# A decoder block on one core: the token norm applied by the transposes, and the first convolution chunk computed in turns over four banks

## The chip, the cores and the metric

The kernel runs on one core of a Trainium2 chip. The metric is the device time of one execution in microseconds (us); the smaller the better. The engines of the core work side by side, each through its own row of instructions in order: TensorE (PE) multiplies, VectorE (DVE), ScalarE (ACT) and GpSimd (POOL) do the elementwise work, SyncE (SP) issues the transfers from memory.

## The reference

The kernel computes one decoder block for 256 tokens of width 1024, in float32. The parts that the change touches stand first.

```python
h = rmsnorm(x, norm_mix_g)
proj = h @ w_in                       # q, k, v, forget gate, conv value a, conv gate
a, gate = split(proj[..., OFF_C:] + b_glu)
z = a * sigmoid(gate)                 # 512 channels
z = depthwise_causal_conv(z, w_dw) + b_dw        # width 31
conv = silu(layernorm(z, ln_g, ln_b))
attn = rmsnorm(forgetting_attention(q, k, v, log_sigmoid(f)))
x = x + concat([attn, conv]) @ w_out
x = x + memory_cross_attention(rmsnorm(x), rmsnorm(mem), w_mq, w_mkv, w_mo)
x = x + hierarchical_moe(rmsnorm(x), ...)        # 4 groups of 8 experts, top 2
out = rmsnorm(x)
```

## The kernel before

**Weights and the ring.** Weights pass through a ring of 15 slots in the on-chip memory. SP issues their loads in the order of `ring.queue`; `ring.pump` issues as many as slots are free, and a slot comes free when PE has used its content. The first conv weights, `("ca", 0)` (value) and `("cg", 0)` (gate), `("ca", 1)` and `("cg", 1)`, are queued first. The normed tokens `xn` hold one slot-sized place until they are transposed.

**Products in three parts.** A float32 product is made of three single-pass ones (`mm3`, L415 to L417): both factors are split into a high and a low part, and high x high, high x low and low x high are added up in a PSUM bank. The weight's split is made by `split` in pieces of 128x512: ACT casts the high part `WH` (L409), and GpSimd, or DVE for every third piece, subtracts for the low part `WL` (L411). The tokens' split is made by `put_split` from a transposed bank: ACT writes the high part (L421), DVE the low part (L422). `hT` is the pair that holds them for the tokens.

**The front.** `normed` computes each token's 1/rms (square sums on ACT and DVE, a Sqrt on ACT, a reciprocal on DVE) and scales the tokens into `xn`; `transposed` transposes `xn` on PE (tile `ht`) in four steps and calls `put_split`. The parameter rows `prow` and `qrow` are transposed on PE (tile `prm_t`) and copied on DVE to `pT` (the taps) and `qTm` (the biases).

**The convolution.** `conv_chunk(c)`, c = 0 and 1, computes 256 value channels (tile `pa`) and 256 gate channels (tile `pg`), each in two banks of 128 channels over 8 steps of j, then a Sigmoid `sg` on ACT and the product `z` on DVE for each bank. All weight products use a rotation of three PSUM banks. The 31 taps of each of the four channel blocks then run on DVE, one instruction each (L509 the first, L512 the rest, accumulating in `cacc`), dealt out between DVE's other work by `some_taps`; the last tap of a block writes `y`, and `ysum` adds up the blocks (L515, on DVE for the last). They end when `ln_mean` wants `ysum`: PE's product `mu` (L706) loads it as weights.

**What follows.** v with the forget gate (`pv`, `fS` on DVE at L554), q and k, the memory's norm, the attention, the memory's values (`pmv`, in an order for PE written out by hand, in which `ln_mean` and `ln_rest` stand), the output projection `xo`, the cross attention, the routing, and eight groups of four experts whose weights are streamed. The order of each engine's row outside the hand-written places is set when the kernel is built, by a scheduler with priorities.

## Time and profile before

| | |
|---|---|
| median of 3 runs | 687.4 us (685.74 to 687.7) |
| the profiled execution, its own time | 686.98 us |
| its span, first to last instruction | 685.3 us |
| PE busy | 595.5 us, 87% of the span |
| DVE busy | 224.2 us, 33% |
| ACT busy | 173.0 us, 25% |
| GpSimd busy | 119.1 us, 17% |
| mean granted clock of TensorE | 0.963 |
| moved by DMA | 237.35 MB, 346 GB/s over the span |

The span is what the profile sees; 1.7 us of the execution's time lie outside it. Busy shares are averages over stages that have different limits, so they do not say what sets the time. A granted clock of 1.00 in a stretch means TensorE's higher rate (2.4 GHz), 0.50 its lower one (1.2 GHz).

### The profile page before, as it was taken

To read this page: it belongs to the slowest core of one execution; us is meant where nothing else is said; L and a number is where in the kernel's file an instruction comes from. 1 tells how busy PE (TensorE), PEld (TensorE's weight loads), DVE (VectorE), ACT (ScalarE), POOL (GpSimd) and SP (SyncE) were. 2 spreads that over 40 slices of the span, in tenths; PEclk is the share of its full clock that TensorE was granted. 3 is DMA by queue.
4 is the path that set the end of the run, shared out by engine and by line. 5 is a ranking of instruction groups with operands and counts; after the bars stand their busy time and mean duration, and the time that the engine had idled before them with its cause. 6 is when DMAs were issued, how large, how long until landed. Compare 5 with 4: busy or idle time off the path is not lost. (4 is left out here: it accounts for less than half of the span.)

```text
span 685.3 us, 8873 instructions
## 1 busy us (share of the span) xinstructions
PE 595.5 (87%) x3497; PEld 353.1 (52%) x3497; DVE 224.2 (33%) x489; ACT 173.0 (25%) x375; POOL 119.1 (17%) x106
## 2 busy tenths in 40 slices
PE   7999999998999999999768968976895788789775
PEld 5999889876998852625312612521261243125122
DVE  5699879887775630400000100000010000001013
ACT  6576675574654510000000000000000000000004
POOL 4546425674333200000000000000000000000000
PEclk9999999999999999999989989998999899899898
DMA  7979550555966999999999999999999999999993
GB/s 247 358 184 364 209 193 2 184 185 191 361 232 221 395 360 421 420 418 419 420 420 418 421 419 420 419 421 419 421 418 421 419 420 419 421 419 418 421 398 116
DMA packets 65163, 237.35 MB, mean 346 GB/s; under 512 B 11852, under 2 KB 31456, under 8 KB 42080
## 3 DMA queue, kind: packets, MB, share of 16 engines
q1 hardware_dynamic: 64832, 235.72, 87.6%
q10 hardware_dynamic: 288, 1.05, 0.4%
q8 instruction: 28, 0.46, 0.3%
q14 instruction: 15, 0.12, 0.0%
HBM read 235.70 MB, written 1.05 MB: 345 GB/s over the span
## 5 line engine op out<-in xcount | busy, mean ns | idle before, releaser
L1311 PE MATMUL eu<-w,tg 128*32 128x512 f32 x512 | 105.3, 715 | 43.9 <-DMA w<-in_w_up 43.9
L411 POOL TENSOR_TENSOR WL<-w,WH 128x512 fp32r<-128x512 f32 (+1 forms) x80 | 109.2, 1375 | 110.7 <-ACT WH L409 94.9
L1339 PE MATMUL ed<-w,hT 128*32 128x512 f32 x448 | 86.5, 597 | 15.4 <-DMA w<-in_w_down 10.6
L1311 PEld LDWEIGHTS eu<-w,tg 128*32 128x32 f32 x512 | 22.3, 126 | 123.0 <-DMA w<-in_w_up 78.8
L409 ACT CAST WH<-w 128x512 fp32r<-128x512 f32 (+1 forms) x120 | 72.9, 619 | 46.6 <-PE pmk L416 7.3
L998 POOL TENSOR_SCALAR SR<-S,r 128x128 f32<-128x128 f32 x7 | 4.2, 605 | 388.2 <-PE Y L1050 337.3
L1034 DVE TENSOR_TENSOR sgm<-sgm,eu 128x512 f32<-128x512 f32 x8 | 5.5, 688 | 192.7 <-PE eu L1311 164.6
L1016 PEld LDWEIGHTS tgp<-SR,X 128*128 128x128 f32 x256 | 62.0, 335 | 12.0 <-ACT SR L997 9.5
L1016 PE MATMUL tgp<-SR,X 128*128 128x128 f32 x256 | 63.8, 405 | 3.6 <-ACT SR L997 3.6
L1339 PEld LDWEIGHTS ed<-w,hT 128*32 128x32 f32 x448 | 22.2, 109 | 74.6 <-issue 37.4
L512 DVE SCALAR_TENSOR_TENSOR cacc<-z,pT,cacc 128x256 f32<-128x256 f32 x116 | 56.4, 486 | 2.6
L1311 PE MATMUL eg<-w,tg 128*32 128x512 f32 x448 | 53.8, 594 | 0.8 <-DMA w<-in_w_gate 0.8
L1004 DVE TENSOR_TENSOR S<-S,GT 128x256 f32<-128x256 f32 x8 | 3.4, 425 | 126.4 <-POOL SR L998 126.3
L1040 ACT COPY hT<-hTp 128x512 f32<-128x512 f32 x8 | 4.7, 586 | 152.2 <-PE hTp L1037 152.2
L411 DVE TENSOR_TENSOR WL<-w,WH 128x512 fp32r<-128x512 f32 (+1 forms) x40 | 36.4, 911 | 11.0 <-ACT WH L409 10.7
L1033 ACT ACTIVATE sgm<-eg 128x512 f32<-128x512 f32 x8 | 4.8, 597 | 128.3 <-PE eg L1311 112.2
L1311 PEld LDWEIGHTS eg<-w,tg 128*32 128x32 f32 x448 | 16.9, 109 | 30.6 <-issue 22.4
L1048 ACT COPY yd<-ed 128x512 f32<-128x512 f32 x14 | 8.2, 586 | 93.8 <-PE ed L1339 93.8
L1017 DVE TENSOR_TENSOR tg<-tgp,g_norm_ffn_g 128x512 f32<-128x512 f32 (+2 forms) x19 | 11.5, 607 | 53.0 <-PE tgp L1016 53.0
L1050 PE MATMUL Y<-yd,GST 128*128 128x512 f32 x56 | 25.9, 605 | 0.0
L415 PE MATMUL pmk<-w,WH 128*128 128x256 f32 x64 | 18.8, 294 | 0.0
L416 PE MATMUL pmk<-w,WH 128*128 128x256 f32 x64 | 18.5, 290 | 0.0
(353 smaller groups left out, 976.4 us busy)
## 6 DMA issues: line engine op xcount, KB each, us to landing
w<-in_w_gate SPq DMA_DIRECT2D x64, 1024.0 KB, 19.9
w<-in_w_up SPq DMA_DIRECT2D x64, 1024.0 KB, 19.9
w<-in_w_down SPq DMA_DIRECT2D x63, 1024.0 KB, 19.9
w<-in_w_mkv SPq DMA_DIRECT2D x8, 1024.0 KB, 12.8
w<-in_w_in SPq DMA_DIRECT2D x7, 1024.0 KB, 10.5
w<-in_w_out SPq DMA_DIRECT2D x4, 1024.0 KB, 9.4
w<-in_w_mq SPq DMA_DIRECT2D x4, 1024.0 KB, 13.2
w<-in_w_mo SPq DMA_DIRECT2D x4, 1024.0 KB, 5.5
```

What stands on the lines that cost most here:

```text
L409: A.copy(hi, src)
L411: (V if nsplit[0] % 3 == 0 else G).tensor_tensor(lo, src, hi.bitcast(F32), op=OP.subtract)
L415: T.matmul(o, L[0], R[0], start=first, stop=False)
L416: T.matmul(o, L[0], R[1], start=False, stop=False)
L512: V.scalar_tensor_tensor(dst, z[:, cb, t:t + S], pT[:, 4 * t + cb:4 * t + cb + 1], acc, op0=OP.mult, op1=OP.add)
L1016: T.matmul(t[:, j], X[:, i, ja + j::NJ], SR[:, i], start=i == 0, stop=i == NT - 1)
L1017: V.tensor_tensor(tg[:, ja:ja + step], t, gff[:, ja:ja + step].unsqueeze(2).to_broadcast([P, step, n]), op=OP.mult)
L1034: V.tensor_mul(sg, sg, pu[0:n])
L1048: ins = A.copy(yd[:, :w], pd[0:n, :w])
L1050: T.matmul(outs[i], GST[:, i], yd[:, :w], start=first, stop=last)
L1311: T.matmul(o[32 * q:32 * q + 32], tg[:, j, 32 * q:32 * q + 32], ws[q][0][:, jj], start=j == 0, stop=j == NJ - 1, tile_position=(0, 32 * q))
L1339: T.matmul(os_[n][32 * q:32 * q + 32], hh[:, j, 32 * q:32 * q + 32], ws[q][0][:, jj, 512 * n:512 * n + 512], start=j == 0, stop=j == 3, ti ...
```

## The change

Eight things change together.

1. `xn` and `normed` go. `scaled_ident(i)` makes a 128x128 diagonal of 1/rms for each half of the tokens (in `y[:, 3]`, which is not in use yet), and `h_transposes` multiplies the raw tokens with it: a float32 product that transposes and scales at once. The ring's place of `xn` is free from the start.
2. The first chunk's value and gate weights load straight into two slots, in six transfers that take turns (j 0 to 1, 2 to 3, 4 to 7 of each), ahead of the parameter rows; the second chunk's follow those.
3. The first chunk is written out in a hand-made order for PE, ACT and DVE. For m = 0 to 3, it splits two j of the tokens, one piece of value weights (`sa`, low part on GpSimd) and one of gate weights (`sb`, low part on DVE), and multiplies both pieces, so value and gate are accumulated side by side in four banks (two of the rotation `mm`, two of the scores' `sc`). The tokens' transposes for m + 2 follow the products of m.
4. The parameter transposes and the copies `pT` and `qTm` stand behind the products of m = 2.
5. The Sigmoid table is loaded right behind the second Sqrt instead of at the first Sigmoid.
6. The second chunk's value product takes its banks in turns from `mm` and from `tr`.
7. 12 instead of 16 warm-up products at the start, and three more between the transposes.
8. `Ring.pump` issues each load in one piece, the first too.

```diff
 NWARM2 = 5
-NWARM0 = 16
+NWARM0 = 12
...
-    xn, xn_pool = ring.spare((NT, D))
     hT, mT = Pair(ring), Pair(ring)
 
     def qcols(key, view, c0, n):
         ring.queue(key, (NJ, n), view[:, :, c0:c0 + n])
 
-    for c in range(2):
-        qcols(("ca", c), winv, OFF_C + 256 * c, 256)
-        qcols(("cg", c), winv, OFF_C + DC + 256 * c, 256)
+
+    w0 = [ring.spare((NJ, 256)) for _ in range(2)]
+    for j0, j1 in ((0, 2), (2, 4), (4, 8)):
+        for (v, _), c0 in zip(w0, (OFF_C, OFF_C + DC)):
+            nc.sync.dma_start(v[:, j0:j1], winv[:, j0:j1, c0:c0 + 256])
+    for key, c0 in (("ca", OFF_C), ("cg", OFF_C + DC)):
+        qcols((key, 1), winv, c0 + 256, 256)
...
+    ring.pump(2)
     gain("mem_norm_g", "(p k) -> p k", "mem_norm_g")
-    ring.pump(4)
+    ring.pump(2)
...
-    def split(v):
+    def split(v, eng=None):
...
-                (V if nsplit[0] % 3 == 0 else G).tensor_tensor(lo, src, hi.bitcast(F32), op=OP.subtract)
+                (eng or (V if nsplit[0] % 3 == 0 else G)).tensor_tensor(lo, src, hi.bitcast(F32), op=OP.subtract)
...
-    def normed(src, dst):
-
-        for i in range(NT):
-            ss = small.tile([P, 2], F32, tag="nrmss", name="nrmss")
-            ssq(ss[:, 0:1], src[:, i, :D // 2], A)
-            ssq(ss[:, 1:2], src[:, i, D // 2:], V)
-            r = small.tile([P, 1], F32, tag="nrmr1", name="nrmr1")
-            V.tensor_add(r, ss[:, 0:1], ss[:, 1:2])
-            A.activation(r, r, AF.Sqrt, scale=1.0 / D, bias=eps_t)
-            V.reciprocal(r, r)
-            A.activation(dst[:, i, :D // 2], src[:, i, :D // 2], AF.Copy, scale=r)
-            V.tensor_scalar(dst[:, i, D // 2:], src[:, i, D // 2:], r, None, op0=OP.mult)
+    def scaled_ident(i):
+
+        ss = small.tile([P, 2], F32, tag="nrmss", name="nrmss")
+        ssq(ss[:, 0:1], X[:, i, :D // 2], A)
+        ssq(ss[:, 1:2], X[:, i, D // 2:], V)
+        r = small.tile([P, 1], F32, tag="nrmr1", name="nrmr1")
+        V.tensor_add(r, ss[:, 0:1], ss[:, 1:2])
+        A.activation(r, r, AF.Sqrt, scale=1.0 / D, bias=eps_t)
+        V.reciprocal(r, r)
+        t = y[:, 3, i * P:(i + 1) * P]
+        V.tensor_scalar(t, ident, r, None, op0=OP.mult)
+        return t
...
-    normed(X, xn)
-    transposed(hT, xn, gvec["norm_mix_g"], 0, NJ, strided, "h")
-    ring.done(xn_pool)
-    t = tr_ps("prm_t")
-    T.transpose(t[:, 0:P], prow, ident)
-    T.transpose(t[:, P:P + 20], qrow, ident[0:20, 0:20])
-    V.tensor_copy(pT, t[:, 0:P])
-    V.tensor_copy(qTm, t[:, P:P + 20])
-
...
-    def conv_chunk(c):
-        pa = wstat(("ca", c), hT, "pa")
-        pg = wstat(("cg", c), hT, "pg")
+    def conv_glu(c, pa, pg):
         for b in range(2):
             cb = 2 * c + b
             sg = cvp.tile([P, S], F32, tag="sg", name="sg", bufs=2)
             A.activation(sg, pg[b], AF.Sigmoid, bias=b_glu[:, 4 + cb:5 + cb])
             V.scalar_tensor_tensor(z[:, cb, CW - 1:], pa[b], b_glu[:, cb:cb + 1], sg, op0=OP.add, op1=OP.mult)
 
-    conv_chunk(0)
-    conv_chunk(1)
+
+    ht = [None] * (NJ // 2)
+
+    def h_transposes(rI, i, k2):
+        if i == 0:
+            ht[k2] = tr_ps("ht", (P, 2, S))
+        for kk in range(2):
+            T.matmul(ht[k2][:, kk, i * P:(i + 1) * P], X[:, i, strided(2 * k2 + kk)], rI[i], start=True, stop=True)
+
+    ET = mybir.EngineType
+    with tc.manual_schedule(engines={ET.PE, ET.Activation, ET.DVE}):
+        rI = [scaled_ident(0)]
+        for k2 in range(2):
+            h_transposes(rI, 0, k2)
+        keep_warm(onesb, 2)
+        rI.append(scaled_ident(1))
+        for k2 in range(2):
+            h_transposes(rI, 1, k2)
+        keep_warm(onesb, 1)
+        pa = [mm_ps("pa", (P, S)) for _ in range(2)]
+        pg = [sc_ps("pg", (P, S)) for _ in range(2)]
+        sa, sb = split(w0[0][0], G), split(w0[1][0], V)
+        A.preload_act_table(AF.Sigmoid)
+        for m in range(NJ // 2):
+            if m == 0:
+                ap = next(sa)
+            for kk in range(2):
+                put_split(hT, 2 * m + kk, ht[m][:, kk], gvec["norm_mix_g"][:, 2 * m + kk:2 * m + kk + 1])
+            if m > 0:
+                ap = next(sa)
+            for o, piece in ((pa, lambda: ap), (pg, lambda: next(sb))):
+                piece = piece()
+                for b in range(2):
+                    bs = slice(b * P, (b + 1) * P)
+                    for j, hi, lo in piece:
+                        mm3(o[b], (hi[:, bs], lo[:, bs]), hT.both(j), j == 0, j == NJ - 1)
+            if m + 2 < NJ // 2:
+                for i in range(NT):
+                    h_transposes(rI, i, m + 2)
+            if m == 2:
+                t = tr_ps("prm_t")
+                T.transpose(t[:, 0:P], prow, ident)
+                T.transpose(t[:, P:P + 20], qrow, ident[0:20, 0:20])
+                V.tensor_copy(pT, t[:, 0:P])
+                V.tensor_copy(qTm, t[:, P:P + 20])
+        conv_glu(0, pa, pg)
+        ring.done(w0[0][1], w0[1][1])
+
+    banks = cycle((mm_ps, tr_ps))
+    pa = wstat(("ca", 1), hT, "pa", bank=lambda name, shape: next(banks)(name, shape))
+    conv_glu(1, pa, wstat(("cg", 1), hT, "pg"))
```

Where it moves instructions on DVE, in two places. The first is the front, from the tokens' first split to the first tap. `w` is the tokens' pair (lo parts at L422, in the kernel after L420), `prm_t` the parameter transposes, `z` the first GLU. DVE's row before:

```order
15 L422 SCALAR_TENSOR_TENSOR w<-ht,g_norm_mix_g,w 128x256 x4
16 L411 TENSOR_TENSOR WL<-w,WH 128x512
17 L422 SCALAR_TENSOR_TENSOR w<-ht,g_norm_mix_g,w 128x256 x2
18 L498 COPY pT<-prm_t 128x128
19 L422 SCALAR_TENSOR_TENSOR w<-ht,g_norm_mix_g,w 128x256
20 L499 COPY qTm<-prm_t 128x20
21 L411 TENSOR_TENSOR WL<-w,WH 128x512
22 L535 SCALAR_TENSOR_TENSOR z<-pa,qTm,sg 128x256
23 L509 TENSOR_SCALAR cacc<-z,pT 128x256
```

The same place after the change:

```order
15 L420 SCALAR_TENSOR_TENSOR w<-ht,g_norm_mix_g,w 128x256 x2
16 L409 TENSOR_TENSOR WL<-w,WH 128x512
17 L420 SCALAR_TENSOR_TENSOR w<-ht,g_norm_mix_g,w 128x256 x2
18 L409 TENSOR_TENSOR WL<-w,WH 128x512
19 L567 COPY pT<-prm_t 128x128
20 L568 COPY qTm<-prm_t 128x20
21 L420 SCALAR_TENSOR_TENSOR w<-ht,g_norm_mix_g,w 128x256 x2
22 L409 TENSOR_TENSOR WL<-w,WH 128x512 x3
23 L522 SCALAR_TENSOR_TENSOR z<-pa,qTm,sg 128x256
24 L498 TENSOR_SCALAR cacc<-z,pT 128x256
```

Before, one lo part stood behind pT's copy and none behind qTm's. Now both copies stand ahead of the two lo parts of m = 3 (row 21), and three WL pieces in place of one follow before the first z.

The second place is where the taps end. `att` takes PE's attention output `po`, `pmv` is the memory's values, `y` is a block's last tap, and `mu` the mean that PE makes of `ysum`. Around the second att, before:

```order
113 L512 SCALAR_TENSOR_TENSOR cacc<-z,pT,cacc 128x256 x4
114 L512 SCALAR_TENSOR_TENSOR y<-z,pT,cacc 128x256
115 L509 TENSOR_SCALAR cacc<-z,pT 128x256
116 L512 SCALAR_TENSOR_TENSOR cacc<-z,pT,cacc 128x256 x4
117 L679 TENSOR_TENSOR att<-po,rr 128x512
118 L411 TENSOR_TENSOR WL<-w,WH 128x512
```

After:

```order
114 L501 SCALAR_TENSOR_TENSOR cacc<-z,pT,cacc 128x256 x8
115 L501 SCALAR_TENSOR_TENSOR y<-z,pT,cacc 128x256
116 L715 TENSOR_TENSOR att<-po,rr 128x512
117 L498 TENSOR_SCALAR cacc<-z,pT 128x256
118 L409 TENSOR_TENSOR WL<-w,WH 128x512
119 L501 SCALAR_TENSOR_TENSOR cacc<-z,pT,cacc 128x256
```

A first tap and four taps stood ahead of att and stand behind it. At the end of the taps, before:

```order
141 L512 SCALAR_TENSOR_TENSOR cacc<-z,pT,cacc 128x256 x6
142 L411 TENSOR_TENSOR WL<-w,WH 128x512
143 L512 SCALAR_TENSOR_TENSOR y<-z,pT,cacc 128x256
144 L515 TENSOR_TENSOR ysum<-ysum,y 128x256
145 L730 COPY w<-pmv 128x512
146 L411 TENSOR_TENSOR WL<-w,WH 128x512
147 L707 SCALAR_TENSOR_TENSOR y<-mu,y 128x1024
```

After:

```order
141 L501 SCALAR_TENSOR_TENSOR cacc<-z,pT,cacc 128x256 x7
142 L409 TENSOR_TENSOR WL<-w,WH 128x512
143 L501 SCALAR_TENSOR_TENSOR cacc<-z,pT,cacc 128x256 x4
144 L501 SCALAR_TENSOR_TENSOR y<-z,pT,cacc 128x256
145 L766 COPY w<-pmv 128x512
146 L504 TENSOR_TENSOR ysum<-ysum,y 128x256
147 L409 TENSOR_TENSOR WL<-w,WH 128x512
148 L743 SCALAR_TENSOR_TENSOR y<-mu,y 128x1024
```

The copy of `pmv` stands ahead of `ysum` now, and the taps that moved behind att show here as four more ahead of `y`.

## Rows read from the trace of the kernel before

**Rows 1.** Windows: us, PE, PEld, DVE, ACT, POOL busy (instructions), PEclk, DMA share, GB/s.

```profile
225.00:230.00 5.00, 5.00 (x27) 4.05 (x25) 2.55 (x7) 3.58 (x13) 2.58 (x2) 1.00 0.97 385
```

**Rows 2.** Waits of SP, 226 to 668 us: total, times, longest.

```profile
SPq L122 <- DMA w<-in_w_up: 115.0, 55, 3.5
```

**Rows 3.** Waits of PE, 39 to 220 us.

```profile
PE xo L417 <- DVE w L720: 1.5, 1, 1.5
PE pq L415 <- DVE fS L554: 0.7, 1, 0.7
```

**Rows 4.** Waits of PE, 5 to 39 us.

```profile
PE pg L415 <- ACT sg L534: 1.1, 2, 0.6
```

**Rows 5.** Timeline of PE in the experts: start, us, instructions.

```profile
242.82 3.12 PE L1016 MATMUL tgp<-SR,X 128*128 128x128 f32 x12 [0.18 <-ACT SR L997]
```

**Rows 6.** Timeline of ACT: first casts, and a table load.

```profile
8.42 1.12 ACT L409 CAST WH<-w 128x512 fp32r<-128x512 f32 x2
...
40.36 1.28 ACT L539 ACT_TABLE_LOAD   x1
41.66 0.63 ACT L409 CAST WH<-w 128x520 fp32r<-128x520 f32 x1
```

**Rows 7.** Groups by line, 4 to 27 us: count, busy, mean ns, idle before.

```profile
L411 POOL TENSOR_TENSOR WL<-w,WH 128x512 fp32r<-128x512 f32 x8 | 10.6, 1345 | 14.7 <-ACT WH L409 10.2 <-DVE cacc L512 4.5
...
L422 DVE SCALAR_TENSOR_TENSOR w<-ht,g_norm_mix_g,w 128x256 fp32r<-128x256 f32 x8 | 3.6, 475 | 2.6 <-ACT w L421 2.6
...
L498 DVE COPY pT<-prm_t 128x128 f32<-128x128 f32 x1 | 0.3, 291 | 1.2 <-PE prm_t L497 1.2
```

**Rows 8.** Timeline of PE, the convolution's chunks.

```profile
9.97 0.50 PE L415 MATMUL pa<-w,WH 128*128 128x256 f32 x2 [0.34 <-ACT w L421]
...
26.86 0.28 PE L415 MATMUL pa<-w,WH 128*128 128x256 f32 x1
...
32.74 0.28 PE L415 MATMUL pg<-w,WH 128*128 128x256 f32 x1
...
35.44 0.28 PE L417 MATMUL pg<-w,WL 128*128 128x256 f32 x1
...
39.22 0.28 PE L415 MATMUL pv<-WH,w 128*128 128x260 f32 x1
```

**Rows 9.** Timeline of DVE, from the first z to fS.

```profile
23.92 0.48 DVE L535 SCALAR_TENSOR_TENSOR z<-pa,qTm,sg 128x256 f32<-128x256 f32 x1 [2.06 <-ACT sg L534]
24.44 0.55 DVE L509 TENSOR_SCALAR cacc<-z,pT 128x256 f32<-128x256 f32 x1
...
26.95 1.72 DVE L411 TENSOR_TENSOR WL<-w,WH 128x512 fp32r<-128x512 f32 x1 [0.40 <-ACT WH L409]
...
31.34 0.68 DVE L411 TENSOR_TENSOR WL<-w,WH 128x512 fp32r<-128x512 f32 x1
31.94 5.21 DVE L512 SCALAR_TENSOR_TENSOR cacc<-z,pT,cacc 128x256 f32<-128x256 f32 x10
...
52.24 0.17 DVE L554 TENSOR_TENSOR fS<-pv,bfor 128x8 f32<-128x8 f32 x1
```

**Rows 10.** Timeline of DVE, from att to the end of the taps.

```profile
109.60 0.69 DVE L679 TENSOR_TENSOR att<-po,rr 128x512 f32<-128x512 f32 x1 [0.68 <-PE po L674]
110.60 0.69 DVE L411 TENSOR_TENSOR WL<-w,WH 128x512 fp32r<-128x512 f32 x1 [0.31 <-ACT WH L409]
...
131.28 1.01 DVE L515 TENSOR_TENSOR ysum<-ysum,y 128x256 f32<-128x256 f32 x1
132.22 0.68 DVE L730 COPY w<-pmv 128x512 f32<-128x512 f32 x1
```

**Rows 11.** Tile mu: its weight loads.

```profile
L706 PEld LDWEIGHTS mu<-ysum,ones x2: 189/189/189, 133.4 to 133.6; 128*128 128x128 f32 x2
```

**Rows 12.** Windows of half clock; columns as in rows 1.

```profile
12.70:16.10 3.40, 3.38 (x16) 3.40 (x17) 1.95 (x4) 2.35 (x5) 1.81 (x2) 0.50 0.63 181
...
159.50:162.80 3.30, 3.30 (x10) 2.52 (x9) 3.30 (x5) 0.62 (x1) 1.87 (x2) 0.50 0.78 246
```

7 lines of the change are left out of this document (1 added, 6 removed).

## The prediction

> **What bounds the kernel now.** I read the windows first, from the end backwards, to see how far from the end a microsecond counts. From about 225 us on the DMA engines are full (share 0.97 at 385 GB/s in 225 to 230) while PE is busy too, [rows 1]; in that half of the program SP's queue, which issues the expert weights, spends 115.0 us in 55 waits for in_w_up alone, [rows 2]. So the expert stage takes what its bytes take, and the time is set by when its stream begins. It begins when ring slots come free, and those are freed by PE's products of the stages before. A shift of PE anywhere before 225 us therefore goes to the end one to one, unless a later wait swallows it.
>
> Next come PE's waits between 39 and 220 us, [rows 3]. There are few. Two matter: the second half of q's product waits 0.7 us for fS, a DVE result, and the output projection waits 1.5 us for the end of the convolution's LayerNorm (DVE, L720). So at two places PE is met by DVE's static order, and there it is DVE that decides. A gain ahead of the first counts only as far as fS comes earlier too; a loss ahead of LayerNorm counts whole.
>
> Before 39 us PE waits twice for a Sigmoid, 1.1 us together, [rows 4].
>
> **Part 1, the norm, and the first chunk up to 21 us.** ACT and DVE lose the normalising passes over the tokens; instead a 128x128 diagonal is made and 16 fp32 products take the transposes' place. Their price in the trace is 12 in 3.12 us, 0.26 each, [rows 5], the transposes' too within 0.03. Ahead of the first WH cast, ACT now has the Sigmoid table. Before, the first cast begins at 8.42, [rows 6]; it stood behind two normalising passes and two Sqrts. Without them ACT is through the second Sqrt at about 7.24 (my hand chain: its square sum stands one such pass earlier in ACT's row), and the load of 1.28 ends at 8.52. Then WH 0.6, and in turn hi0, lo0, hi1, lo1 at 0.47 each (lo's row, [rows 7], taken for hi too, which has the same shape), because hi1 and lo0 read one bank and the put_split calls take them in turns: the last ends at 11.02. The third product of each j also needs GpSimd's WL, 1.35 us behind WH, which is there by 10.5. So PE runs densely from about 11.05, where before pa began at 9.97 and then stuttered.
>
> A product's pitch is (35.44 - 32.74)/23 = 0.1175 us, [rows 8]; 24 of them, one m, take 2.82. Products of m0 less the four already done end at 13.4, transposes for m2 0.95, m1 2.81, transposes for m3 0.95, m2 2.81: 20.9, and the parameter transposes make it 21.2.
>
> **Part 2, a new stall.** In DVE's row the copies pT and qTm now stand ahead of the lo pieces of m3 (rows 19 to 21 of the order), and they wait for PE's parameter transposes, which stand behind all 24 products of m2. Behind them, in a line: pT 0.29, qTm at most that, say 0.17, lo6 0.47, hi7 0.47 on ACT (same bank, in turns), then the WH cast of the last piece, 0.63, which ACT has behind hi7, then GpSimd's WL 1.35. From 21.2 that gives 24.5 to 24.6 for the third product of m3: PE stands still for about 3.3 us. The remaining 22 products end at 27.1. Before, chunk 0 ended at 26.86. What chunk 0 gained by fewer waits the stall takes away.
>
> **Part 3, chunk 1 with four banks.** From 26.86 to 39.22 before, 12.36 us; 96 products at 0.1175 are 11.28, so it held 1.1 of waiting, most of it for the Sigmoid that frees a bank. After: 27.1 + 11.3 = 38.4, 0.8 earlier. But the first v product's second bank now waits for the last z, about 0.4. PE would reach fS at about 51.0, where it came 0.7 before fS's end (51.7).
>
> DVE's side: z0 was at 23.92 and fS at 52.24, [rows 9], 28.3 us with 37 taps, 2 first taps and 6 WL. z0 moves to about 28.45 (pg's end at 27.1, Sigmoid 0.47, and two WL ahead of it on DVE). Between z0 and fS the new row has 33 taps and 5 WL: four taps at 0.52 (10 in 5.21) less is 2.1, and of WL one less, 0.7 to 1.7. A WL on DVE takes 0.68 where GpSimd is idle and 1.72 where GpSimd runs one too: 1.05 more for each that meets one. Before, two met. With none meeting, fS comes at 28.45 + 28.3 - 2.1 - 0.7 - 2.1 = 51.85; of the 0.40 that DVE idled for a WH cast I take half away: 51.65 where it was 52.24. **Term 1 = -0.6**, since the half of q behind it starts with its end. Bounds: -0.7 if PE decides (it would be there at 51.0, 0.7 before), +1.5 if two meet, +2.6 if three.
>
> **Part 4, the tail of the taps.** DVE waits for att(1) from PE at 109.60, idle 0.68, [rows 10]. Taps ahead of that place cost nothing, taps behind it do. The order now has one first tap and four taps more behind it, and the copy w<-pmv ahead of ysum. The first tap takes 0.55 but 0.31 of it falls in the wait before the next WL, and the rows overlap a little: 0.1 to 0.25. Four taps are 2.1. y's last tap ended at 131.25 and ends now at 133.45; copy 0.6; ysum 0.45 to 1.0 (1.01 in the trace, where GpSimd ran beside it). Ready at 134.5 to 135.05. PE loads ysum as weights for mu at 133.4, [rows 11]; in the trace before ysum was there 1.1 earlier. PE waits 1.1 to 1.65, I take 1.4 by the middle, and everything behind mu (the LayerNorm chain with its 1.5 us wait) moves along: **term 2 = +1.4**. Bounds 0 (if the ysum add doesn't meet and taps overlap more) and 1.7. All of it is relative to att(1), so term 1 shifts both sides and doesn't change it.
>
> **The clock.** Granted clock was 0.50 in 12.70 to 16.10, behind a stretch in which PE stuttered, and 0.50 again in 159.50 to 162.80, behind the LayerNorm waits, [rows 12]. Each costs half its length, 1.7 us. The first should not come at that place, which the dense counting of part 1 already has at full rate; the stall of part 2 may bring it back between 25 and 29. Then chunk 1 ends 1.7 later, PE comes to q's second half at 52.7, and the difference to term 1 is +0.85. The second stays.
>
> **Sum.** 686.98 (the profiled run) - 0.6 + 1.4 = 687.8, a change of +0.8. The median of the runs shown is 0.4 above the profiled run, so 688.2 stands against 687.4. About 0.3%, 2.1 us, is what a measurement of this kernel can tell from no change: **same**.
>
> **Rivals.**
> - **GpSimd meets DVE (slower).** DVE's WL casts between z0 and fS run into GpSimd's. The order alone doesn't decide it; it hangs on ACT's pace. One meeting gives +0.4 + 1.4 = 689.2 against the median and is still the same; from two on, +1.5 + 1.4, it is 690.3, three 691.4. For it: two of six met before. Against: fewer casts there, and the taps between them are the same. Chance 0.25.
> - **The stall of part 2 isn't there (faster).** If DVE could pass the copies, m3 would follow m2, chunk 0 would end at 23.9, z0 at 25.2 and fS at 48.5; PE would be there by then: -4.0 + 1.4 gives 684.8. It decides from a stall under about 1.6 us. Against it: each engine takes its row in order, and prm stands behind m2's products on PE. Chance 0.12.
> - **Half rate behind the stall (same).** +0.85: 689.1. For it: both stretches at 0.50 come behind idle time of PE. Chance 0.07.
> - **The LayerNorm stretch keeps full rate.** PE's longer wait at mu changes where the clock looks; -1.65 gives 686.6, the same, and faster only with the mu wait gone as well (685.2). Chance 0.07, of which 0.03 faster.
> - **The table switch costs more than its load.** In the trace the cast behind the load starts at 41.66, where the load of 40.36 ends (1.28), [rows 6]. If a wait of the load's own length (1.28) came behind it, the front would be 1.3 later throughout, term 1 become +0.7 and the time 689.5, at the edge of slower. Chance 0.04. The Trainium skill (page "ScalarE: Activation LUTs", section "What ACT_TABLE_LOAD costs") says that every switch costs a drain of some 1380 ns beside a load of 1283 ns; by that page this rival would be the rule, the load agrees with the row, the drain doesn't show behind it.
>
> **How the numbers follow.** The forecast has 0.45. Faster: 0.12 + 0.03 = 0.15. Slower: 0.25, with the table's edge 0.02 more. The rest, 0.58, is the same: forecast, half rate, one meeting. The range leaves out about one in ten on each side: below, a bit of the rival at 684.8; above, three meetings. So 685.0 to 690.7; the forecast's own is 687.0 to 689.3.
>
> **What would show it.** A wait of PE of 2.5 to 3.5 us before m3's products, with DVE's pT copy waiting for prm just before; no wait of pg for sg in chunk 1; z0 near 28.5 and fS near 51.7; WL rows of 0.68 and not 1.7 on DVE in between; PE waiting 1.1 to 1.7 us for ysum at mu, where it waited for nothing; the same waits behind it; and an expert stage that is only moved. I am wrong if PE is at q's second half before 50 or after 53.5, or if mu doesn't wait.

## The result, and the profile after

The changed kernel takes 693.14 us (median of 11 runs, 690.81 to 697.26), the kernel before 685.96 in 11 runs beside them (683.57 to 688.95). The ratio is 1.0099, 95% interval [1.0076, 1.0121]: slower by some 7 us, beyond the upper end of the forecast range. The profiled execution took 693.68 with a span of 691.8 us; the kernel before had 686.98 and 685.3. The difference of the two spans, 6.5, is what the rows have to explain. Two single runs of kernels below took far longer than the others of their kernel (726.95 and 1699.29 us); they are left out.

PE's timeline of the changed kernel shows where its stages begin. Columns: start, us, engine, line, tiles, count, and idle time before with its releaser.

```profile
11.10 0.38 PE L413 MATMUL pa<-w,WH 128*128 128x256 f32 x1
...
14.08 2.07 PE L531 MATMUL ht<-y,X 128*128 128x128 f32 x8
...
18.83 2.07 PE L531 MATMUL ht<-y,X 128*128 128x128 f32 x8
...
23.59 0.28 PE L565 MATMUL prm_t<-ident,prow 128*128 128x128 f32 x1
...
25.90 0.58 PE L413 MATMUL pa<-w,WH 128*128 128x256 f32 x1 [1.87 <-ACT WH L407]
...
27.28 0.58 PE L415 MATMUL pa<-w,WL 128*128 128x256 f32 x1 [0.59 <-POOL WL L409]
...
32.13 0.41 PE L413 MATMUL pa<-w,WH 128*128 128x256 f32 x1
...
43.73 0.39 PE L413 MATMUL pv<-WH,w 128*128 128x260 f32 x1
...
55.37 0.29 PE L413 MATMUL pq<-w,WH 128*128 128x256 f32 x1
...
153.25 0.39 PE L413 MATMUL xo<-WH,w 128*128 128x512 f32 x1
...
250.71 0.50 PE L1052 MATMUL tgp<-SR,X 128*128 128x128 f32 x1 [0.18 <-ACT SR L1033]
```

The product at 32.13 is chunk 1's first, 5.3 later than before (26.86, [rows 8]); the first of v is 4.5 later (39.22). The output projection `xo` began at 144.20 before and is 9.05 later. The first product of the experts, `tgp`, is 7.9 later (242.82, [rows 5]). From there to the end the changed kernel took 441.1 us and the kernel before 442.5. Over all profiled executions of this study that stretch took 440.7 to 444.2 (440.7 in the changed kernel's second one), so the 1.4 us that come back there lie within what executions differ by.

PE's waits from 44 to 225 us in the changed kernel, beside [rows 3] (total, times, longest):

```profile
PE pq L413 <- DVE fS L590: 1.7, 1, 1.7
PE xo L415 <- DVE w L756: 1.5, 1, 1.5
PE var L750 <- DVE w L420: 1.1, 1, 1.1
PE mu L742 <- DVE ysum L504: 1.0, 1, 1.0
```

The wait of 1.5 is the old one. That for fS grew from 0.7, that at mu is new, and that at var (`ln_mean`'s second product) was 0.3 before.

DVE's timeline of the changed kernel, around the places where PE meets it:

```profile
24.06 0.29 DVE L567 COPY pT<-prm_t 128x128 f32<-128x128 f32 x1 [3.96 <-PE prm_t L566]
24.27 0.17 DVE L568 COPY qTm<-prm_t 128x20 f32<-128x20 f32 x1
24.36 0.47 DVE L420 SCALAR_TENSOR_TENSOR w<-ht,g_norm_mix_g,w 128x256 fp32r<-128x256 f32 x1
25.37 0.48 DVE L420 SCALAR_TENSOR_TENSOR w<-ht,g_norm_mix_g,w 128x256 fp32r<-128x256 f32 x1 [0.54 <-ACT w L419]
26.39 3.06 DVE L409 TENSOR_TENSOR WL<-w,WH 128x512 fp32r<-128x512 f32 x2 [0.54 <-ACT WH L407]
...
31.60 0.48 DVE L522 SCALAR_TENSOR_TENSOR z<-pa,qTm,sg 128x256 f32<-128x256 f32 x1 [0.47 <-ACT sg L521]
...
57.81 0.17 DVE L590 TENSOR_TENSOR fS<-pv,bfor 128x8 f32<-128x8 f32 x1
...
116.52 0.69 DVE L715 TENSOR_TENSOR att<-po,rr 128x512 f32<-128x512 f32 x1 [1.96 <-PE po L710]
...
140.23 0.68 DVE L766 COPY w<-pmv 128x512 f32<-128x512 f32 x1
140.83 0.86 DVE L504 TENSOR_TENSOR ysum<-ysum,y 128x256 f32<-128x256 f32 x1
141.61 1.76 DVE L409 TENSOR_TENSOR WL<-w,WH 128x512 fp32r<-128x512 f32 x1
143.30 1.21 DVE L743 SCALAR_TENSOR_TENSOR y<-mu,y 128x1024 f32<-128x1024 f32 x1
```

Windows of the changed kernel, columns as in [rows 1]: behind the stall, at 80 us, and at the place of the LayerNorm stretch of [rows 12].

```profile
24.60:28.00 3.40, 1.52 (x5) 1.22 (x6) 2.31 (x4) 3.06 (x6) 1.82 (x2) 0.68 1.05 348
28.00:31.40 3.40, 3.40 (x18) 3.40 (x17) 2.29 (x2) 0.92 (x2) 2.59 (x2) 0.50 1.09 350
80.50:83.80 3.30, 3.30 (x16) 3.08 (x16) 0.49 (x2) 1.89 (x4) 2.14 (x2) 0.50 0.00 0
167.40:170.80 3.40, 2.74 (x12) 2.27 (x13) 3.40 (x5) 0.69 (x2) 2.56 (x2) 1.00 0.47 131
```

Together, in us: the front +5.3; chunk 1 on four banks -0.8; the fS wait +1.0; half rate at 80 us +1.4; mu +1.0; var +0.85 (a WL subtraction ahead of it takes 1.76 instead of 0.68, beside one on GpSimd); half rate at the LayerNorm, which before had and this execution hadn't, -1.2; small pieces +0.35; the experts -1.4. That is +6.5, the difference of the spans.

### The profile page after: what moved, and what is told of

It reads as the page before. It is cut to its first block, busy times and chain, and to the rows that moved or that the text cites. A ratio compares the mean times of both kernels' runs of the same rounds, so it can differ in the third digit from the quotient of the medians.

```text
span 691.8 us, 8902 instructions
## 1 busy us (share of the span) xinstructions
PE 600.8 (87%) x3512; PEld 358.1 (52%) x3512; DVE 227.1 (33%) x491; ACT 171.8 (25%) x373; POOL 116.6 (17%) x104
## 5 line engine op out<-in xcount | busy, mean ns | idle before, releaser
L1347 PE MATMUL eu<-w,tg 128*32 128x512 f32 x512 | 101.5, 703 | 42.8 <-DMA w<-in_w_up 42.8
L409 POOL TENSOR_TENSOR WL<-w,WH 128x512 fp32r<-128x512 f32 (+1 forms) x78 | 106.7, 1375 | 119.7 <-ACT WH L407 98.9
L1375 PE MATMUL ed<-w,hT 128*32 128x512 f32 x448 | 89.0, 598 | 16.2 <-DMA w<-in_w_down 11.5
L409 DVE TENSOR_TENSOR WL<-w,WH 128x512 fp32r<-128x512 f32 (+1 forms) x42 | 38.0, 908 | 10.5 <-ACT WH L407 10.2
```

Of the source, the lines that this page charges most:

```text
L409: (eng or (V if nsplit[0] % 3 == 0 else G)).tensor_tensor(lo, src, hi.bitcast(F32), op=OP.subtract)
L1347: T.matmul(o[32 * q:32 * q + 32], tg[:, j, 32 * q:32 * q + 32], ws[q][0][:, jj], start=j == 0, stop=j == NJ - 1, tile_position=(0, 32 * q))
L1375: T.matmul(os_[n][32 * q:32 * q + 32], hh[:, j, 32 * q:32 * q + 32], ws[q][0][:, jj, 512 * n:512 * n + 512], start=j == 0, stop=j == 3, ti ...
```

## The experiments

Three theories stood at first. **Front**: the loss is the stall behind the parameter copies, with half clock behind it. **Norm**: it is the fp32 products that took the transposes' place. **DVE**: whatever the front does, the row of 124 taps ends too late for mu. One reading decides much of what follows: the second att, att(1) for short. There DVE waits for PE's `po` in both kernels (0.68 us before, [rows 10], and 1.96 above), so what stands ahead of it in DVE's row has been done in time, and `ysum` ends a length behind it that comes of what DVE's order holds between the two: 22.7 us before (109.60 to 132.29, [rows 10]), 25.2 in the changed kernel (116.52 to 141.69). DVE waits for `po` there in every kernel below that leaves att in its place (0.6 to 2.3 us). Each ratio below stands against runs of the kernel before beside it.

### The parameter transposes behind m3 (on the changed kernel)

```diff
-            if m == 2:
+            if m == 3:
                 t = tr_ps("prm_t")
```

> The parameter transposes and DVE's two copies move from behind m = 2 to behind m = 3; nothing else of the source changes. Theory (the front lost its time to the stall that these copies make and to the half clock behind it): no wait of PE ahead of m = 3, no stretch of half clock there, the second chunk's first product at about 27 instead of 32.1, and the whole 3 to 5 us under the changed kernel, about 688 to 690, not more because the order now puts still more taps behind att, so that PE's wait at mu grows to about 3 us. Rival A (DVE's row up to fS is the bound): the second chunk starts 5 us earlier, but PE's wait for fS grows from 1.7 to 5 or more, and the whole moves by less than 1.5 us. Rival B (the clock falls because of the float32 products, not because of the stall): half clock comes anyway and the second chunk starts at about 29.

Measured: 690.96 us, ratio 1.0073 [1.0046, 1.0100]. PE's timeline:

```profile
23.45 0.28 PE L415 MATMUL pg<-w,WL 128*128 128x256 f32 x1
23.57 0.28 PE L413 MATMUL pa<-w,WH 128*128 128x256 f32 x1
23.68 0.28 PE L414 MATMUL pa<-w,WH 128*128 128x256 f32 x1
24.38 0.39 PE L415 MATMUL pa<-w,WL 128*128 128x256 f32 x1 [0.41 <-POOL WL L409]
...
27.45 0.39 PE L413 MATMUL pa<-w,WH 128*128 128x256 f32 x1
```

The stall is gone but for 0.41, and chunk 1 begins 4.7 earlier than in the changed kernel. Little of it arrives: PE's waits from 44 us now read

```profile
PE mu L742 <- DVE ysum L504: 2.7, 1, 2.7
...
PE pq L413 <- DVE fS L590: 0.6, 1, 0.6
```

and xo is still 3.9 late. So the stall is real, and the whole came down by 2.2 us of the 3 to 5 expected. `ysum` ended 4.3 earlier, but PE came to the memory's values, ahead of mu, 6.0 earlier (120.69 against 126.67). DVE's timeline says why:

```profile
110.55 0.69 DVE L715 TENSOR_TENSOR att<-po,rr 128x512 f32<-128x512 f32 x1 [1.95 <-PE po L710]
...
136.42 0.97 DVE L504 TENSOR_TENSOR ysum<-ysum,y 128x256 f32<-128x256 f32 x1
```

DVE waits for PE at att(1) as long as it did, and `ysum` ends 26.8 behind it instead of 25.2. The edit moved two transposes in the source, but the scheduler dealt the taps anew: two taps and one WL subtraction more stand behind att(1) now. The longer wait at mu is this kernel's order, as its expectation had it, and not an old loss come to light.

### PE kept busy during the stall (on the changed kernel, run in two sets)

```diff
                 T.transpose(t[:, P:P + 20], qrow, ident[0:20, 0:20])
+                wb = mm_ps("warm")
+                for _ in range(12):
+                    T.matmul(wb, onesb, onesb.unsqueeze(1).to_broadcast([P, 4, P]), start=True, stop=True)
```

> The changed kernel with twelve warm-up products on PE right behind the parameter transposes, in the free third bank; their results are used by nothing. Theory: the stall ahead of m = 3's third product is as long as before (it ends at about 27.3), but PE works through most of it, the granted clock stays at 1.00, m = 3 takes 2.6 instead of 4.7 us, the second chunk starts at about 30.1 instead of 32.1, and the whole is about 2 us under the changed kernel. Rival A (DVE up to fS is the bound): PE's wait for fS grows by those 2 us and the whole stays within 0.7. Rival B (the float32 products pull the clock down): half clock comes at the same place and nothing is gained.

> The run with the warm-up products behind the parameter transposes once more, for a second profile and more times. Theory (the half clock behind the stall is PE's idle time's work): m = 3 at full clock again, the second chunk's first product at 29.9 to 30.1, and over more executions 1 to 2 us under the changed kernel's 693.1. Rival (in the first profile the clock stayed up by chance): half clock behind the stall in this profile, and the time equal to the changed kernel's within 0.5.

Measured: 693.14 us, 1.0103 [1.0070, 1.0136], and 691.91, 1.0075 [1.0053, 1.0096]. The windows of the first show the same stall at full clock:

```profile
24.00:27.40 3.40, 3.08 (x15) 1.55 (x15) 2.32 (x5) 2.60 (x6) 1.29 (x1) 1.00 1.10 348
27.40:30.80 3.40, 3.40 (x30) 3.40 (x30) 3.40 (x3) 2.37 (x5) 3.25 (x3) 1.00 1.09 350
```

Chunk 1 began at 29.91 and 30.20, 2.2 and 1.9 before the changed kernel's: that is what half rate cost there in the trace. All five profiled executions that keep the stall and leave PE idle in it have half rate behind it (the changed kernel twice, and below the norm alone, the changed kernel with a later att and with eight taps fewer); neither of the two with the filling has. In the time it is at most half shown: one ratio is no better, the other's interval overlaps the changed kernel's. In both, the wait at mu is 1.0 and `ysum` ends 25.2 behind att(1), as in the changed kernel, though att(1) comes 4.7 and 2.9 us earlier.

### The norm back as it was, alone and with the first edit

```diff
-        t = y[:, 3, i * P:(i + 1) * P]
-        V.tensor_scalar(t, ident, r, None, op0=OP.mult)
+        A.activation(xn[:, i, :D // 2], X[:, i, :D // 2], AF.Copy, scale=r)
+        V.tensor_scalar(xn[:, i, D // 2:], X[:, i, D // 2:], r, None, op0=OP.mult)
...
-            T.matmul(ht[k2][:, kk, ...], X[:, i, strided(2 * k2 + kk)], rI[i], start=True, stop=True)
+            T.transpose(ht[k2][:, kk, ...], xn[:, i, strided(2 * k2 + kk)], ident)
```

> The changed kernel with the tokens' norm done as before: ACT and DVE scale the tokens into a ring place and PE transposes them with the identity; banks, order and parameter transposes stay. Theory (a float32 product costs twice what the forecast took, 0.49 against 0.25 for a transpose): the products of m = 2 end 1.8 to 2.4 us earlier (about 21.4 instead of 23.6), the stall and the half clock remain, the second chunk starts at about 29.8 to 30.3, and the whole is about 2 us under the changed kernel. Rival (the diagonal's price is hidden or given back by ACT's and DVE's normalising passes): the second chunk starts within 0.7 us of 32.1.

> Both edits together: parameter transposes behind m = 3, and the tokens' norm done as before with plain transposes. Theory: the effects add up, the second chunk starts at about 24.7 to 25.2, full clock, and the whole is 5 to 7.5 us under the changed kernel, about 685.5 to 688, near the kernel before, with what is left of the loss at mu (a wait of about 3 us). Rival A (DVE up to fS is the bound): fS does not come earlier than in the run with the parameter transposes moved alone, and the whole equals that run within 1 us.

Measured: alone 694.21, 1.0108 [1.0072, 1.0143]; with the transposes behind m3 690.29, 1.0059 [1.0040, 1.0077]. Alone it brought nothing: what the transposes save is spent in PE's waits for ACT in the front (2.7 us) and at half rate from 12.6 to 16.0 and 26.2 to 33.1. With the first edit chunk 1 begins at 26.85, as before the change, and mu waits 2.7: the front is repaired and 0.6% remains, 690.29 where 685.5 to 688 was expected. The 2.7 belongs to the order that came with the first edit (`ysum` 26.8 behind att(1) here too); alone, with the changed kernel's order, it is 25.2 and mu waits 1.0. So Front and Norm are not the whole of it in either kernel, but what is left is 1.0 at mu in the one and 2.7 in the other.

### Less for DVE around the LayerNorm (on the last kernel)

DVE subtracts every sixth WL instead of every third from the memory's keys to its values, and ACT copies the first `pmv`.

```diff
-                (eng or (V if nsplit[0] % 3 == 0 else G)).tensor_tensor(lo, src, hi.bitcast(F32), op=OP.subtract)
+                (eng or (V if nsplit[0] % share[0] == 0 else G)).tensor_tensor(lo, src, hi.bitcast(F32), op=OP.subtract)
...
+        if c == 3:
+            share[0] = 6
...
-            (V.tensor_copy if i else A.copy)(vm[:, i, 512 * c:512 * c + 512], os_[i])
+            (V.tensor_copy if i and c else A.copy)(vm[:, i, 512 * c:512 * c + 512], os_[i])
```

> The run with both edits (parameter transposes behind m = 3, norm as before) and, from the last quarter of the memory's keys to the memory's values, every sixth instead of every third subtract on DVE, and the first two copies of the memory's values both on ACT. Between att and ysum DVE then has three subtracts of 0.7 to 1.2 us and one copy of 0.6 less. Theory (what is left of the loss is PE's wait of 2.7 us for ysum, made by what DVE has behind att): ysum comes about 3 us earlier, the wait at mu goes to 0 to 0.3, the products of the output projection start about 2.5 us earlier than in that run, and the whole comes down from 690.3 to about 687.5 to 688. Rival (GpSimd, which now subtracts five of six pieces, becomes late and PE waits for its low parts): waits of PE for GpSimd's subtract in 105 to 145 us, and nothing or less is gained.

Measured: 687.23 us, 1.0021 [1.0007, 1.0034], but hardly by the intended way: mu still waits 2.4. Its front had no half-rate stretch (chunk 1 at 25.62). Of the three subtractions and the copy that left DVE, only 0.3 us arrived (`ysum` 26.6 behind att(1)), since subtractions given to GpSimd came back as slower work on DVE. A tiny operation, while GpSimd subtracts from 111.78 to 116.85, took 0.15 in the kernel that this one was built on, where GpSimd was idle at that moment:

```profile
113.41 0.96 DVE L371 TENSOR_SCALAR anmt<-anmt 128x2 f32<-128x2 f32 x1
```

### The four banks alone, for chunk 1 (on the kernel before)

```diff
+        banks = cycle((mm_ps, tr_ps))
-        pa = wstat(("ca", c), hT, "pa")
+        pa = wstat(("ca", c), hT, "pa", bank=(lambda name, shape: next(banks)(name, shape)) if c else mm_ps)
```

> The kernel before with one part of the change: the second chunk's value product takes its banks in turns from two rotations, so that four banks are in use. Theory (the second chunk's waits for the Sigmoid go, but DVE decides when fS comes): no wait of pg for sg in the second chunk, the first v product 0.6 to 0.9 us earlier than 39.2, but the wait for fS grows by about as much, PE is at the products behind it within 0.4 us of before, and the whole stays within 1.5 us of before; the order has two taps more behind att, so a wait of up to 1 us at mu is possible. Rival (what PE gains in the second chunk goes to the end): everything behind is 0.6 to 0.9 earlier and the whole faster by that.

Measured: 686.63 us, 1.0012 [0.9996, 1.0027]: no difference. The first v product is 2.2 earlier, 1.7 of it a half-rate stretch that this execution lacked; behind fS, for which q now waits 1.6, only 1.0 is left. Faster banks ahead of fS are worth little, as the forecast's two-place argument had it.

### Both kernels once more

> The kernel before, unchanged, for a second profile. Theory (the stretches of half clock around 160 us and in the last 10 us come and go from execution to execution, those behind PE's long waits in the front belong to the kernel): the waits of PE and the times of the stages up to 150 us agree with the first profile within 0.3 us but for a half-clock stretch of 1.7, and the part behind the last bytes differs by up to 2 us. Rival (all half-clock stretches belong to the kernel): the same stretches at the same places within 0.5 us.

> The changed kernel, unchanged, for a second profile. Theory: the stall ahead of m = 3 and the half clock behind it (about 6.8 us long) come again, the second chunk starts at 32 within 0.5 us; the stretch around 80 us may be absent, which makes the expert stage start 1.7 us earlier. Rival (the half clock behind the stall is chance as well): m = 3 takes 2.6 us, and the second chunk starts at about 30.

Measured: 687.31 and 690.96 us, one execution each. Before repeats within 0.1 us at every stage from chunk 1 to tgp. The changed kernel does not: tgp is at 248.34, 2.4 earlier than in its first profile. Its windows:

```profile
27.30:30.60 3.30, 3.30 (x15) 3.30 (x16) 2.45 (x3) 1.25 (x3) 3.12 (x2) 0.50 1.09 350
80.50:83.80 3.30, 3.30 (x30) 3.30 (x30) 2.08 (x6) 2.81 (x6) 2.14 (x2) 1.00 0.00 0
```

Half rate behind the stall came again, but for half as long, and the stretch at 80 us was absent. These account for 0.7 and 1.4 of the 2.4; the waits at mu and var (1.0 and 1.1) are the same. So the mu wait is no accident of one execution, and the stretch at 80 us is: one like it, at 75 us, came also in single executions of the kernel before with the four banks and with eight taps more.

### att(1) later in DVE's row (on the norm-restored kernel, on the first edit, on the changed kernel)

DVE idles 1.96 us at att(1). Here it first does the taps up to the 93rd.

```diff
+            with tc.issue_after(tap_ins[92].ins) if i else ExitStack():
                 V.tensor_tensor(att[:, i]...)
```

and the copy of the first `pmv` goes to ACT, as above.

> The run with both edits (parameter transposes behind m = 3, norm as before), and DVE's att of the second half held back until the third tap of the last block, so that the taps fill the 1.9 us in which DVE idles for PE there; the first two copies of the memory's values both on ACT. GpSimd's share of the subtracts stays. Theory (what DVE does behind att makes ysum late, and DVE can only be helped by work that leaves it or fills its idle time, since work given to GpSimd slowed DVE by as much): about 2.5 us less on DVE between po and ysum, the wait at mu 0 to 0.5 instead of 2.7, and the whole 2 to 3 us under that run's 690.3: 687.3 to 688.3; with the stretches of half clock absent a little below the kernel before. Rival (ysum is bound by the sum of DVE's work from the first z on, not by what stands behind att): the wait at mu stays above 1.5 us and the whole within 1 us of 690.3.

> The same two edits at att and the copies, on the kernel that keeps the diagonal and has only the parameter transposes moved behind m = 3. Theory (a diagonal's product costs 0.23 us more than a transpose, eight of them stand between the products of the first chunk): chunk 1 starts 1.8 us later than with plain transposes at the same clock, at 27.45, PE's stages behind it stay 1.2 to 1.8 us later, and the whole is 1 to 2 us above the run with plain transposes, about 689. Rival (DVE's row up to fS and ysum decides, the transposes' price is hidden): the same time as the run with plain transposes within 0.7.

> The changed kernel with only the two edits at att and the copies; the front stays as it is. Theory (the order of DVE's row at the end of the taps costs about 1.9 us of the 7: 1.0 at mu and 0.85 at var): no wait at mu, the wait at var back to 0.3, the output projection starts 1.5 to 2 us earlier relative to the memory's values, and the whole is 1.3 to 2 us under the changed kernel: about 691.3. Rival (the waits at mu and var only replace a wait further on): the output projection's waits grow by as much and the whole stays within 0.7 of 693.1.

Measured, in this order: 688.58, 1.0027 [1.0014, 1.0040]; 690.43, 1.0062 [1.0040, 1.0084]; 694.35, 1.0130 [1.0105, 1.0155]. On the changed kernel it made things no better, and mu waits 2.3 instead of 1.0: the theory that the idle place at att costs the microseconds fails. The timelines of the first say why:

```profile
107.86 0.62 ACT L408 CAST WH<-w 128x512 fp32r<-128x512 f32 x1 [1.72 <-PE pmk L415]
...
108.51 0.69 DVE L410 TENSOR_TENSOR WL<-w,WH 128x512 fp32r<-128x512 f32 x1 [1.91 <-ACT WH L408]
...
111.14 0.68 DVE L720 TENSOR_TENSOR att<-po,rr 128x512 f32<-128x512 f32 x1
```

The idle time went to the next instruction, whose WH cast waits for PE as well. In the first two mu still waits 2.7. The first's better time comes with an earlier PE (pmv at 117.69 against 120.14), not with a shorter wait at mu.

The first two differ in the norm alone, and their profiles are alike in the rest: neither has half rate ahead of 159 us, and mu waits 2.7 in both. Chunk 1 begins at 27.64 with the fp32 products and at 25.84 with the transposes, and the 1.8 us reach pmv (119.49 against 117.69), xo (146.98 against 145.15) and, as 1.9, the medians (the two intervals just touch). This is the price of the diagonal by itself; the expectation of 1 to 2 us holds, its rival (within 0.7) does not.

### Eight taps fewer, and eight more

In the changed kernel the last block loses eight taps; in the kernel before it gets eight twice. The values of that block are then others, the shapes are the same.

```diff
-        for t in range(1, CW):
+        for t in range(9 if cb == 3 else 1, CW):
...
-        for t in range(1, CW):
+        for t in (list(range(1, 9)) if cb == 3 else []) + list(range(1, CW)):
```

> The changed kernel without eight taps of the last channel block (of 124 in all; the convolution of that block lacks them). Theory (DVE's row from the first z to ysum has a fixed length and makes ysum late): ysum comes 4.2 us earlier relative to PE, the wait at mu is 0, the one at var 0.3 to 1.1, the output projection starts 1 to 1.9 us earlier relative to the memory's values than in the changed kernel, and the whole is 1 to 2 us under its 693.1. Rival (PE's waits at mu and var come from the order of single instructions): a wait of 1 us or more stays at mu, the whole within 0.7.

> The kernel before with eight taps of the last channel block done twice (its output is another). Theory: in the kernel before ysum is there 1.1 us before PE wants it, and everything that makes DVE's row longer beyond that goes to the end: 8 x 0.52 = 4.2 more on DVE, a wait of 3.1 to 3.7 us at mu, the stages behind it as much later, the whole at about 689.4. Rival (DVE has slack that takes it up): a wait at mu under 1 us and the whole within 1 us of 686.2.

Measured: the changed kernel with fewer 692.36, 1.0097 [1.0062, 1.0131]; the kernel before with more 689.52, 1.0040 [1.0021, 1.0059]. PE's waits, first with fewer (no row of mu), then with more:

```profile
PE pq L413 <- DVE fS L590: 1.7, 1, 1.7
...
PE var L750 <- DVE w L420: 0.3, 1, 0.3
```

```profile
PE mu L706 <- DVE ysum L515: 3.2, 1, 3.2
```

In the second, PE is within 0.6 us of before as far as pmv. `ysum` ends 27.3 behind att(1) instead of 22.7, which made a wait of 3.2 at a place that had a margin of 1.1 ([rows 10, 11]; 1.4 by the 4.6 more and the wait), and 2.7 us in the time. Its execution had half rate behind that wait (136.4 to 143.3), so its later stages are no measure. The first is half a result: in the trace both waits fall (pmv is 4.7 late and xo 4.7, no more; in the changed kernel's second profile, with pmv at 124.34 against 124.43, xo is 2.0 later), but the time hardly moved; 1.9 us, 0.27%, would be expected of it, and the interval holds that as well as nothing.

### Channel block 0 first (on the norm-restored kernel, and on the first edit)

All products of block 0 before those of block 1, so that z0 can begin halfway.

```diff
+        pcs = {(o, b): split(w0[o][0][:, :, b * P:(b + 1) * P], (G, V)[o]) for b in range(2) for o in range(2)}
...
+            products(m, 0, (ap, gp))
...
+        glu_block(0, 0, pa, pg)
+        for m in range(NJ // 2):
+            products(m, 1, nx if m < 2 else nx2)
+        glu_block(0, 1, pa, pg)
```

> The run with both edits (parameter transposes behind, norm as before, still four banks and the hand-made order), with the first chunk's weights cut by channel block instead of by j: value and gate of the first 128 channels are multiplied first over all of m, then the parameter transposes, copies, Sigmoid and z of that block, then the other 128 channels. Same products, casts and subtracts. Theory (the first z sets when DVE's row of some 108 us ends): first z at 20 to 22 instead of 28.5, fS without a wait, ysum at 129 to 131, no wait at mu, the expert stage 1 to 3 us earlier than in the kernel before and the whole 683.5 to 685.5. Rival (the wait at mu comes from how DVE is loaded behind att, not from the first z): the wait at mu stays at 2 to 2.7 us and the whole at about 690.

> The same cut by channel block on the kernel that keeps the diagonal. Theory: first z at 21 to 24, no wait at mu, the whole within 2 us above the run with plain transposes: 684 to 687, at or under the kernel before. Rival: the float32 products between the first block's products hold PE and the first z back as in the changed kernel, and the wait at mu is 1 us or more.

Measured: 689.53, 1.0044 [1.0025, 1.0062], and 690.86, 1.0074 [1.0047, 1.0101]. In the first z0 came at 22.84, earlier than before the change, and mu waits no more. But `ysum` ended at 136.55, hardly earlier than with z0 at 28.51, and PE meets DVE in a new place:

```profile
PE pv L414 <- DVE z L521: 2.3, 1, 2.3
```

The loss moved from mu to v. DVE's timeline shows where the early z0 went:

```profile
113.84 0.69 DVE L731 TENSOR_TENSOR att<-po,rr 128x512 f32<-128x512 f32 x1 [1.61 <-PE po L726]
```

DVE waits for PE at att(1) here too. `ysum` ends 22.7 behind it, the same as before the change, and the order behind att(1) again holds 26 taps and five WL subtractions, as before. So the start of z0 does not set the end of the taps, and the wait at mu went with the order.

### DVE relieved for good (on the norm-restored kernel, and on the kernel before)

The attention norm's second square sum, its two scalings and the first `pmv` copy go to ACT; GpSimd gets nothing.

```diff
-            ssq(ss[:, i:i + 1], src[:, i], V if i == 1 else A)
+            ssq(ss[:, i:i + 1], src[:, i], V if i == 1 and name != "anm" else A)
...
-        V.tensor_scalar(att[:, i], att[:, i], ra[:, i:i + 1], None, op0=OP.mult)
+        A.activation(att[:, i], att[:, i], AF.Copy, scale=ra[:, i:i + 1])
```

> The run with both edits (parameter transposes behind m = 3, norm as before), and four pieces of work moved from DVE to ACT between att and ysum: the square sum of att's second half, the two scalings of att, and one copy of the memory's values; the order then has one subtract fewer ahead of ysum too. Theory (DVE's row from the first z to ysum is the bound behind the front): 3 to 4 us less on that row, the wait at mu 0 to 0.4 instead of 2.7, the expert stage starts 0 to 2 us earlier than in the kernel before, and the whole is 685 to 686.5. Rival (ACT, which casts the weights' high parts, becomes late by the work it gets): waits of PE or DVE for ACT's casts between 110 and 145 us, and nothing is gained against 690.3.

> The kernel before with the same four pieces of work moved from DVE to ACT. Theory (there ysum is in time and PE decides when mu is done): ysum comes 2 us or more earlier, PE's stages do not move, the whole within 0.3% of the kernel before. Rival (DVE's row decides there too): the output projection starts 1 us or more earlier and the whole is faster by that.

Measured: 687.09, 0.9996 [0.9979, 1.0014], and 686.32, 0.9999 [0.9983, 1.0015]. On the restored kernel the rows of DVE and PE's waits read

```profile
132.62 0.47 DVE L504 TENSOR_TENSOR ysum<-ysum,y 128x256 f32<-128x256 f32 x1
```

```profile
PE pq L414 <- DVE fS L592: 0.6, 1, 0.6
...
PE var L752 <- DVE w L421: 0.3, 1, 0.3
```

`ysum` ends 22.4 behind att(1) instead of 26.8 (its order has one WL subtraction fewer there, too), 3.8 earlier, mu waits no more, xo is 1.2 behind before's instead of 3.4, and the ratio falls from 1.0059 to 1. The same relief in the kernel before ends ysum 4.2 earlier and moves no stage of PE by more than 0.15 us: there DVE has margin, so it is worth nothing. That pair settles the place. In the traces the first product of the experts comes 2.1 earlier, with a front that is 0.7 later by half rate, which agrees with the wait of 2.7. In the times 1.0059 to 0.9996 is some 4.3 us, but the two intervals are only 1.8 us apart. Neither is a kernel that beats the one before.

## Why the prediction was wrong, by its own steps

Term 1, forecast at -0.6, came out at +5.6: fS ends at 57.98 instead of 52.41. Three steps under it failed: the price of the fp32 product, the small chance of half rate behind the stall, and the path from z0 to fS. Term 2, at mu, held. Times in us; z0, att(1) and the end of `ysum` from DVE's timelines, the wait from PE's waits.

| kernel | z0 | att(1) | end of ysum | ysum behind att(1) | wait at mu | ratio |
|---|---|---|---|---|---|---|
| before | 23.92 | 109.60 | 132.29 | 22.7 | 0 | 1 |
| changed | 31.60 | 116.52 | 141.69 | 25.2 | 1.0 | 1.0099 |
| PE kept busy, first | 31.03 | 111.81 | 136.98 | 25.2 | 1.0 | 1.0103 |
| norm restored alone | 31.24 | 116.50 | 141.67 | 25.2 | 1.0 | 1.0108 |
| parameters behind m3 | 29.10 | 110.55 | 137.39 | 26.8 | 2.7 | 1.0073 |
| the same, norm restored | 28.51 | 110.00 | 136.84 | 26.8 | 2.7 | 1.0059 |
| the last, DVE relieved | 29.21 | 110.72 | 133.09 | 22.4 | 0 | 0.9996 |
| block 0 first, norm restored | 22.84 | 113.84 | 136.55 | 22.7 | 0 | 1.0044 |
| before, 8 taps more | 23.00 | 110.14 | 137.43 | 27.3 | 3.2 | 1.0040 |
| before, DVE relieved | 24.01 | 109.69 | 128.09 | 18.4 | 0 | 0.9999 |

- **Part 1, the price of the fp32 product: this step failed.** "0.26 each" took the twelve records of [rows 5] for twelve products; over the whole of before, `tgp` leaves 256 records for 128 products. The changed kernel has four such products in a step and the trace shows eight records: 2.07 us from start to end, 1.83 until the next product starts at the second step. So one product costs some 0.46, not 0.24 ahead of the next. Two steps of four lie between m0 and the end of m2: 1.76 more than forecast. With m0 ending at 14.08 instead of 13.4 and m1 and m2 taking 0.1 more each, m2 ends at 23.59 instead of 20.9. "The transposes' too within 0.03" was wrong as well: four transposes leave four records and hold PE for 0.37 until the next product (14.94 to 15.31, norm restored with a later att). The two kernels with a later att and the parameters behind m3, which differ in the norm alone, show the exchange at full clock: the two steps cost 2.9 more with the diagonal (1.83 against 0.37 each), but with the old norm m0 ends 0.6 later (14.94 against 14.30), since PE waits 2.3 for ACT in the front, and m1 takes 0.5 longer (3.36 against 2.91). That leaves the 1.8.
- **The table switch** came as counted, a load of 1.28. ACT's timeline of the changed kernel:

```profile
7.22 1.28 ACT L546 ACT_TABLE_LOAD   x1
8.52 0.62 ACT L407 CAST WH<-w 128x512 fp32r<-128x512 f32 x1
```

  The forecast's 7.24 and 8.52 hold to 0.02, and so does the rival's refutation: nothing comes between the load and the cast. The drain that the Trainium skill gives (page "ScalarE: Activation LUTs", section "What ACT_TABLE_LOAD costs") doesn't show here either.
- **Part 2, the stall, was right**: pT, qTm, lo, hi, WH, WL in a line, 3.2 us from 24.06 to 27.28 where 3.3 was forecast; PE has two products to do in it. The place was 2.7 late by part 1.
- **Half rate behind the stall, a rival at 0.07, came in both profiles, and this chance was the second step that failed.** The 22 products behind 27.28 took 4.85 and 4.21 us instead of 2.59, which is 2.3 and 1.6 more where the rival had 1.7, and 1.9 to 2.2 were won in the trace by keeping PE busy. The forecast asked what PE did before the known stretches and then gave its own 3.3 us of idle time a small chance of doing the same.
- **Part 3.** The four banks won 0.8, and 1.0 in the second profile, of the 1.1 forecast. fS did not come at 51.65 but at 57.81, 6.2 later, and PE was at q's second half at 58, past the 53.5 that the prediction had named as a sign of being wrong. Of the 6.2, 5.0 is chunk 1's start (32.13 for 27.1, by the two steps above). The rest, 1.1, is the third step that failed: the forecast counted fS from z0 by DVE's row alone. With the stall away that row does take 22.7 where 23.2 was forecast, but in the changed kernel the last z (45.12) follows PE, 13.0 behind chunk 1's first product (12.9 with the stall away), and comes 13.5 behind z0 instead of 11.2. The rival in which WL subtractions meet GpSimd's between z0 and fS did not happen: they took 0.68 to 0.70 there. They met ahead of z0 (3.06 for two) and behind `ysum` (1.76).
- **Part 4 was right, and so was "All of it is relative to att(1), so term 1 shifts both sides and doesn't change it".** The forecast had `ysum` 24.9 to 25.45 behind att(1), and it ends 25.2 behind. The wait was 1.0 for 1.4, and it is 1.0 in all five executions with this order, while att(1) moves from 111.81 to 116.52. In the table the wait follows the length behind att(1) and not z0: it is what that length has over 24.1. The two kernels with the parameters behind m3 wait 2.7 because their order puts more there. Adding taps makes the wait, relieving DVE takes it away, and relieving DVE where there is margin does nothing: that is shown in the trace, and, all but the eight taps fewer, in the times.
- **Not foreseen**: var's 0.85, a WL subtraction between `ysum` and the LayerNorm that meets GpSimd's.

What stays open: how much of the 7 us in the medians is half rate that comes and goes; why the scheduler deals the taps as it does in each kernel; and how much of the better times of the kernels with every sixth subtraction on DVE and with a later att (0.3% to 0.4% under the one that they were built on, while mu's wait hardly changed) is half rate. Their profiles have one stretch of it ahead of the experts, the other's three, and the first product of the experts comes 2.9 and 2.3 us earlier; one profile each does not show that it is so in the other runs.

## What to carry to other kernels

When a long row of one engine must be finished at a join, find the last place in it where that engine still waited for the other one. What stands ahead of that place costs nothing as long as the wait is there; what stands behind it decides when the join is reached, and the margin is read from there. Here 24.1 us behind att(1) were free: before the change 22.7 were used, and a later or earlier first input changed nothing, while eight taps more came out as a wait of 3.2 us. An edit elsewhere can deal that order anew, so compare the order of every variant before calling a wait that is left the old one. Count the records of an operation against the instructions of the program before dividing a group's time by its count.
